# Taking the first adaLN vectors of a two-layer diffusion backbone off GpSimd

## The chip, the cores and the metric

One core of a Trainium2 chip. The metric is the device time of one execution in microseconds (us), the median of several runs. The engines are TensorE (PE in the profile; PEld its weight loads), VectorE (DVE), ScalarE (ACT), GpSimd (POOL) and SyncE (SP), whose queue issues nearly all the loads.

## The reference

Two layers over 512 latent tokens and 256 context tokens of width 1024, in fp32. Each layer is a half-step SwiGLU feed-forward, a token mixer (differential attention in layer 0, windowed grouped-query attention in layer 1) and a second half-step feed-forward. Every one of the six takes its input normalised and modulated:

```
mod_l = (silu(c) @ ada_w[i] + ada_b[i])          # 9 vectors of 1024 for the latent tokens
mod_c = silu(c_ctx) @ ada_w[i] + ada_b[i]        # 9 for the context tokens
h     = rms(t) * (1 + scale) + shift
t     = t + 0.5 * gate * ((silu(h @ wi_gate) * (h @ wi_up)) @ wo)
```

Nine vectors of 1024 for two kinds of token in each layer are a product of a vector with a 1024 x 9216 matrix. The first feed-forward needs the first two, the shift and the scale (columns 0 to 2047), before it can multiply anything; all others are due later. The change concerns those two.

## The kernel before, in words

Activations stand with the 1024 features on the partitions, as 8 chunks of 128, and the 768 tokens along the row. Every large product is taken three times in fp32r, on a rounded part and its remainder of both operands (`split`, L72: ScalarE rounds, VectorE subtracts; the names are `whi`/`wlo` for weights and `h_h`/`h_l` for activations), which gives VectorE much to do everywhere. The program is written through a framework that sets the order of each engine's instructions from its own estimate of times, so a changed part reorders its neighbourhood; `keep` pins an instruction to the written order on its engine.

**The first phase** runs from the start to the first products of the first feed-forward (L1082 to L1141). It does four things:

- `ada_vectors` (L118) spreads `c` and `c_ctx` over all partitions (`crep`, 128 x 2 x 1024) and applies SiLU.
- The norm: ScalarE squares `x` (L1108), VectorE adds the 8 chunks in a tree (L1111), and `rstd_steps` (L277) sums over the partitions on TensorE (`ps_rt`), takes the power -0.5 on GpSimd (L290), makes a diagonal on VectorE (`dg`, L295) and spreads it with a product with ones (`ps_r`, L303). ScalarE copies that to `rall`. Then `xr<-x,rall` (L1122) is the normalised chunk.
- The vectors, `vectors(k)` (L1118) for each chunk k: `ada_job` (L175) loads a 128 x 1024 slab `araw` and takes one row sum for each kind of token. VectorE does the latent one (L187, multiply with an accumulating sum); GpSimd multiplies for the context one (L190) and ScalarE sums that product (L199). All 8 shifts and the scales of chunks 0, 1, 5 and 7 go this way. The scales of chunks 2, 3, 4 and 6 (`ONPE`) go through `scale_job` (L209): 8 products on TensorE in which the 128 x 128 weight block stands still and the two conditions (`cvec`, 2 columns) move past it. The slabs share 6 rooms (`FIRST`).
- `feed(k)` (L1124): ScalarE applies shift and scale (L1134), rounds to `h_h` (L1135), VectorE makes `h_l` (L1136). `ffn` (L500) calls it before the 12 products of chunk k of its first step f = 0 (`products`, L519, matmuls on L522): 6 with 512 columns, 6 with 256. The first four of a chunk need `h_h` only, the other eight need `h_l` or `wlo`.

After f = 0, VectorE multiplies gate and up (`sg`, L555), and the steps f = 1 and f = 2 follow as plain products. From f = 3 on the products are taken in Strassen's form (`Seven`, L397), for which VectorE first adds and subtracts the quarters of the activations (`sums`, L411) and of the weights (`s`, L442 to L445). Beside all this `Halves` (L219) computes the later adaLN vectors on VectorE, six half slabs `wh` per step (L253).

Of the kernel before, what the change touches and what calls it, by code (L numbers as in the profile page):

```python
# [17 lines left out]
P = 128  # L18
D = 1024
# [23 lines left out]
def hybrid_backbone_kernel(ctx: ExitStack, tc: tile.TileContext, I, out):  # L43
# [10 lines left out]
    def one(name, tag="one"):  # L54
        return ps1.tile([P, 512], F32, name=name, tag=tag)
# [62 lines left out]
    def ada_vectors(pool):  # L118

        crep = pool.tile([P, 2, D], F32, name="crep")  # L120
        for ty, nm in enumerate(("c", "c_ctx")):
            nc.sync.dma_start(crep[:, ty], I[nm].partition_broadcast(P))
            nc.scalar.activation(crep[:, ty], crep[:, ty], AF.Silu)
        nc.sync.dma_start(adab, I["ada_b"])
        return crep

    def load_x(half):
        s0, n, _, _ = half
        for d in range(0, KC, 4):
            nc.sync.dma_start(x[:, d:d + 4, s0:s0 + n], I["x"][:, d:d + 4, s0:s0 + n])  # L130

    def load_small():
        nc.scalar.dma_start(ident, I["ident"])
# [36 lines left out]


    mods = [[None] * NMOD for _ in range(2)]
    JUNK, PRODS = 3, 3

    def ada_job(l, j, engines, pool, crep, bufs, pin=False):  # L175
        m, d = divmod(j, KC)
        w = pool.tile([P, D], F32, name="araw", tag="araw", bufs=bufs)
        nc.sync.dma_start(w, I["ada_w"][l, j])
        if mods[l][m] is None:
            md = const.tile([P, 2, KC], F32, name=f"mod{l}_{m}")  # L180
            mods[l][m] = md[:, 0], md[:, 1], md
        prods = []
        for ty in range(2):
            acc = mods[l][m][ty][:, d:d + 1]
            if engines[ty] is nc.vector:
                o = pool.tile([P, D], BF16, name="junk", tag="junk", bufs=JUNK)
                i = nc.vector.scalar_tensor_tensor(o, w, 1.0, crep[:, ty], ALU.mult, ALU.mult, accum_out=acc)  # L187
            else:
                pr = pool.tile([P, D], F32, name="aprod", tag="aprod", bufs=PRODS)
                i = nc.gpsimd.tensor_mul(pr, w, crep[:, ty])  # L190
                prods.append((pr, acc))
            if pin:
                keep(i)
        md = mods[l][m][2][:, :, d]

        def finish():
            for pr, acc in prods:
                o = pool.tile([P, D], BF16, name="junk", tag="junk", bufs=JUNK)
                nc.scalar.activation(o, pr, AF.Identity, accum_out=acc)  # L199
            bias = adab[:, l, j:j + 1].broadcast_to([P, 2])  # L200
            if m in (1, 4, 7):
                nc.vector.scalar_tensor_tensor(md, md, 1.0, bias, ALU.add, ALU.add)
            else:
                nc.vector.tensor_add(md, md, bias)
                if m in (2, 8):
                    nc.vector.tensor_scalar_mul(md, md, 0.5)
        return finish

    def scale_job(k, pool, bufs):  # L209

        w = pool.tile([P, D], F32, name="araw", tag="araw", bufs=bufs)
        nc.sync.dma_start(w, I["ada_s"][k])
        ps = one("ps_a", "acc")[:, :2]
        for i in range(KC):
            nc.tensor.matmul(ps, w[:, i * P:(i + 1) * P], cvec[:, i], start=i == 0, stop=i == KC - 1)
        bias = adab[:, 0, KC + k:KC + k + 1].broadcast_to([P, 2])
        return lambda: nc.vector.scalar_tensor_tensor(mods[0][1][2][:, :, k], ps, 1.0, bias, ALU.add, ALU.add)

    class Halves:  # L219

# [871 lines left out]
    cvec = start.tile([P, KC, 2], F32, name="cvec")  # L1092
    nc.sync.dma_start(cvec, I["cvec"])
    nc.scalar.activation(cvec, cvec, AF.Silu)
    crep = ada_vectors(start)
    md = const.tile([P, 2, KC], F32, name="mod0_1")
    mods[0][1] = md[:, 0], md[:, 1], md
    with tc.tile_pool(name="f0", bufs=1) as pool:
        load_small()
        for hf in range(2):  # L1100
            load_x(all_[hf])
        xr = [pool.tile([P, T], F32, name="xr", tag=("ah", "al")[d % 2], bufs=5) for d in range(KC)]
        rall = pool.tile([P, T], F32, name="rall", tag="ah", bufs=5)
        steps = []
        for s0, n, _, _ in all_:
            tk = slice(s0, s0 + n)
            for d in range(KC):
                nc.scalar.activation(xr[d][:, s0:s0 + n], x[:, d, s0:s0 + n], AF.Square)  # L1108
            for step in (1, 2, 4):
                for d in range(0, KC, 2 * step):  # L1110
                    nc.vector.tensor_add(xr[d][:, s0:s0 + n], xr[d][:, s0:s0 + n], xr[d + step][:, s0:s0 + n])  # L1111
            steps.append(rstd_steps(xr[0][:, tk], n, D, lambda pr, _, tk=tk: nc.scalar.copy(rall[:, tk], pr), pool))
        for z in zip(*steps):
            for step in z:
                step()
        rest = {}

        def vectors(k):  # L1118
            rest[k] = [ada_job(0, k, (V, G), start, crep, FIRST, pin=k == 0),
                       scale_job(k, start, FIRST) if k in ONPE else  # L1120
                       ada_job(0, KC + k, (V, G), start, crep, FIRST, pin=k == 0)]
            keep(nc.vector.tensor_mul(xr[k], x[:, k], rall))  # L1122

        def feed(k):  # L1124

            if k == 0:
                for f in rest.pop(0):
                    f()
            if 0 < k < KC - 1:
                vectors(k + 1)  # L1130
            hi, lo = h0.reg.hi[:, k], h0.reg.lo[:, k]
            for s0, n, ty, _ in all_:
                sh, sc = (mods[0][i][ty][:, k:k + 1] for i in range(2))
                nc.scalar.activation(xr[k][:, s0:s0 + n], xr[k][:, s0:s0 + n], AF.Identity, bias=sh, scale=sc)  # L1134
            nc.scalar.copy(hi, xr[k])  # L1135
            nc.vector.tensor_sub(lo, xr[k], hi.bitcast(F32))  # L1136
            for f in rest.pop(k + 1, ()):
                f()
        vectors(0)
        vectors(1)  # L1140
        h1 = Norm(0, 3, T, "right", "h1_")  # L1141

        def up_done():
            h0.reg.close()
            h1.open()
        halves.add(0, (2,))
# [135 lines left out]
```

## Time and profile before

| | |
|---|---|
| median of 3 runs | 2940.08 us (2938.19 to 2943.32) |
| the profiled execution | 2939.59 us, of which the span from first to last instruction is 2937.8 us |
| TensorE busy | 2733.8 us (93%) |
| VectorE busy | 2229.2 us (76%) |
| ScalarE busy | 1229.8 us (42%) |
| GpSimd busy | 498.3 us (17%) |
| mean granted TensorE clock | 0.979 |

The profile is one execution. "Busy" is the time in which an instruction of the engine is under way. A busy VectorE may still be waiting inside an instruction, and successive instructions overlap by some 0.08 us, so what one costs is read from the distance between two starts. Nothing but the first 5% of the span is touched by the change, and only that stretch is looked at closely. Times in the trace count from the start of the span.

### The profile page before, as it was taken

The numbers are of one execution on the slowest core, as the hardware profiler recorded it, in microseconds if no ns is written. First come the engines' busy times: TensorE is split into PE (matmuls) and PEld (weight loads), VectorE is DVE, ScalarE is ACT, GpSimd is POOL, SyncE is SP. The second block draws the span as 40 slices with busy tenths as digits, with TensorE's granted clock in tenths as the row PEclk, the third lists the DMA queues.
The fourth block names the chain that finished last, engine by engine and source line by source line (L and its number), as shares of the span: only waits on it lengthen the run. The fifth ranks groups of instructions, "written<-read, shape, count | busy, mean of one in ns | idle before, by whom it ended". The sixth has DMA issues, their size and how long they took to land.

```text
span 2937.8 us, 47517 instructions
## 1 busy us (share of the span) xinstructions
PE 2733.8 (93%) x17948; PEld 2589.0 (88%) x17948; DVE 2229.2 (76%) x4613; ACT 1229.8 (42%) x3053; POOL 498.3 (17%) x586
## 2 busy tenths in 40 slices
PE   4799899999999989799999989999999999999999
PEld 3698898889999978789999978999998999999999
DVE  7988987877677756877886598787766766488887
ACT  4423222336556644323333343332334566454443
POOL 5300000025433422200000051000002521220000
PEclk9899999999999999899999999999999999999999
DMA  6333433322011022233332223343322101223333
GB/s 209 114 127 129 133 125 101 119 79 73 30 30 34 26 85 73 86 108 115 109 114 65 72 76 115 126 133 112 100 73 89 45 29 30 73 78 101 98 93 101
DMA packets 98709, 266.49 MB, mean 91 GB/s; under 512 B 12592, under 2 KB 16688, under 8 KB 98352
## 3 DMA queue, kind: packets, MB, share of 16 engines
q1 hardware_dynamic: 91968, 251.78, 26.8%
q10 hardware_dynamic: 6512, 11.68, 1.2%
q8 instruction: 141, 2.31, 0.3%
q14 instruction: 88, 0.72, 0.1%
HBM read 256.07 MB, written 7.34 MB: 90 GB/s over the span
## 4 chain that ended last, share of the span: by engine, by line
PE 66%; DVE 22%; issue 4%; DMA 4%; ACT 2%; POOL 1%; SPq 0%; ACTq 0%; DVEq 0%; POOLq 0%
PE ps_up L456 24%; PE ps_dn L569 22%; PE ps_qkv L651 7%; DVE wlo L74 4%; PE ps_dn L728 4%; DVE wh L253 3%; DVE junkh L253 2%; PE ps_av L989 2%; PE ps_up L522 2%; DMA wh<-in_ada_w 2%; DVE xs L369 1%; DMA raw<-in_pre_wi 1%; PE ps_av L825 1%; PE ps_s L781 1%; PE ps_pt L978 1%
## 5 line engine op out<-in xcount | busy, mean ns | idle before, releaser
L73 ACT CAST whi<-raw 128x512 fp32r<-128x512 f32 x556 | 341.4, 620 | 765.5 <-PE ps_dn L569 318.0
L569 PE MATMUL ps_dn<-ah,whi 128*128 128x256 f32 (+1 forms) x1456 | 463.3, 321 | 2.6 <-DVE x L390 1.8
L74 DVE TENSOR_TENSOR wlo<-raw,whi 128x512 fp32r<-128x512 f32 x556 | 402.9, 729 | 79.9 <-ACT whi L73 68.4
L569 PE MATMUL ps_dn<-al,whi 128*128 128x256 f32 (+1 forms) x1456 | 462.0, 319 | 0.1
L569 PE MATMUL ps_dn<-ah,wlo 128*128 128x256 f32 (+1 forms) x1456 | 454.1, 319 | 0.2 <-DVE wlo L74 0.2
L456 PE MATMUL ps_up<-h_h,whi 128*128 128x384 f32 (+1 forms) x1216 | 400.9, 330 | 38.7 <-ACT whi L73 25.9
L456 PE MATMUL ps_up<-h_h,wlo 128*128 128x384 f32 (+1 forms) x1216 | 394.3, 328 | 12.9 <-DVE wlo L74 12.8
L456 PE MATMUL ps_up<-h_l,whi 128*128 128x384 f32 (+1 forms) x1216 | 397.8, 327 | 0.0
L390 DVE SCALAR_TENSOR_TENSOR x<-ps_dn,mod,x 128x256 f32<-128x256 f32 (+1 forms) x442 | 241.9, 556 | 142.5 <-PE ps_dn L569 101.9
L73 ACT CAST whi<-s 128x512 fp32r<-128x512 f32 x304 | 188.1, 620 | 266.9 <-PE ps_up L456 221.9
L569 PEld LDWEIGHTS ps_dn<-ah,whi 128*128 128x128 f32 x1456 | 276.1, 191 | 25.3 <-ACT whi L73 2.5
L569 PEld LDWEIGHTS ps_dn<-al,whi 128*128 128x128 f32 x1456 | 277.5, 191 | 19.6 <-DVE al L74 0.3
L569 PEld LDWEIGHTS ps_dn<-ah,wlo 128*128 128x128 f32 x1456 | 275.9, 191 | 19.4 <-DVE wlo L74 0.4
L456 PEld LDWEIGHTS ps_up<-h_h,whi 128*128 128x128 f32 x1216 | 233.1, 192 | 47.1 <-ACT whi L73 27.2
L456 PEld LDWEIGHTS ps_up<-h_h,wlo 128*128 128x128 f32 x1216 | 232.2, 192 | 15.1 <-DVE wlo L74 15.0
L74 DVE TENSOR_TENSOR wlo<-s,whi 128x512 fp32r<-128x512 f32 x304 | 208.2, 687 | 41.7 <-ACT whi L73 38.0
L456 PEld LDWEIGHTS ps_up<-h_l,whi 128*128 128x128 f32 x1216 | 233.0, 192 | 0.5
L651 PE MATMUL ps_qkv<-whi,h_h 128*128 128x256 f32 x704 | 205.4, 292 | 4.3 <-DVE a L607 3.6
L651 PE MATMUL ps_qkv<-wlo,h_h 128*128 128x256 f32 x704 | 199.7, 286 | 1.9 <-DVE wlo L74 1.9
L651 PE MATMUL ps_qkv<-whi,h_l 128*128 128x256 f32 x704 | 200.3, 285 | 0.0
L257 POOL TENSOR_TENSOR mod<-mod,part 128x16 f32<-128x16 f32 (+1 forms) x32 | 14.7, 460 | 1065.4 <-DVE wh L253 1031.5
L253 DVE SCALAR_TENSOR_TENSOR wh<-wh,ch 128x512 f32<-128x512 f32 x256 | 185.5, 733 | 1.7 <-DMA wh<-in_ada_w 1.5
(226 smaller groups left out, 6684.9 us busy)
## 6 DMA issues: line engine op xcount, KB each, us to landing
wh<-in_ada_w SPq DMA_DIRECT2D x256, 256.0 KB, 3.7
raw<-in_pre_wi SPq DMA_DIRECT2D x88, 512.0 KB, 3.5
raw<-in_post_wi SPq DMA_DIRECT2D x88, 512.0 KB, 3.5
raw<-in_pre_wo SPq DMA_DIRECT2D x44, 512.0 KB, 3.5
raw<-in_post_wo SPq DMA_DIRECT2D x44, 512.0 KB, 3.5
raw<-in_a_w_qk SPq DMA_DIRECT2D x16, 512.0 KB, 3.5
araw<-in_ada_w SPq DMA_DIRECT2D x12, 512.0 KB, 4.5
raw<-in_a_w_v SPq DMA_DIRECT2D x8, 512.0 KB, 3.5
```

The costliest lines, as they stand in the source:

```text
L73: nc.scalar.copy(hi, src)
L74: nc.vector.tensor_sub(lo, src, hi.bitcast(F32))
L253: nc.vector.scalar_tensor_tensor(o, w, 1.0, self.c[ty], ALU.mult, ALU.mult, accum_out=self.part[:, ty, d:d + 1])
L369: nc.vector.scalar_tensor_tensor(xs, x[:, d, tk], sc, self.r[p], ALU.mult, ALU.mult)
L390: nc.vector.scalar_tensor_tensor(x[:, d, s0:s0 + n], ps, gate[ty][:, d:d + 1], x[:, d, s0:s0 + n], ALU.mult, ALU.add)
L456: nc.tensor.matmul(ps, ww, z[:, k, :n], start=first and k == 0 and i == 0, stop=k == 3 and i == 2, skip_group_check=True)
L522: nc.tensor.matmul(ps, w, h[:, k, s0:s0 + n], start=k == 0 and i == 0, stop=k == KC - 1 and i == 2)
L569: nc.tensor.matmul(ps, wv, a[:, s0:s0 + n], start=fi == 0 and k == 0, stop=fi == nf - 1 and k == 2)
L651: nc.tensor.matmul(ps, h[:, k, bt], w, start=n == 0, stop=n == 23)
L728: nc.tensor.matmul(ps, wv, o[:, k, s0:s0 + n], start=k == 0 and j == 0, stop=k == KC - 1 and j == 2)
L781: nc.tensor.matmul(sv[:, u], Q[:, c, qt], K[:, c, kb0 * P + u * half:kb0 * P + (u + 1) * half], start=i == 0, stop=i == 1)
L989: nc.tensor.matmul(po[:, j], a[:, k, j], V[:, kb, g], start=k == 0, stop=k == len(kbs) - 1)
```

## The change

All 16 shift sums go to VectorE, two accumulating multiplies a chunk, each chunk's load followed by its sums at once. All 8 scales go to TensorE, and there the operands change places: the two conditions stand still (2 columns of weights) and the 128 columns of the weight block move. The result is a 2 x 128 row, which ScalarE copies out of the accumulator (`row`) and a small product with a 2 x 2 identity turns back into two columns (`ps_b`). GpSimd keeps only the power of the norm. The first two shift slabs are loaded ahead of `x`, the first two scale slabs behind it, all pinned to that order; the slabs have 9 rooms.

```diff
     def load_x(half):
         s0, n, _, _ = half
         for d in range(0, KC, 4):
-            nc.sync.dma_start(x[:, d:d + 4, s0:s0 + n], I["x"][:, d:d + 4, s0:s0 + n])
+            keep(nc.sync.dma_start(x[:, d:d + 4, s0:s0 + n], I["x"][:, d:d + 4, s0:s0 + n]))
...
-    def ada_job(l, j, engines, pool, crep, bufs, pin=False):
-        m, d = divmod(j, KC)
+    def shift_job(k, pool, crep, bufs):
         w = pool.tile([P, D], F32, name="araw", tag="araw", bufs=bufs)
-        nc.sync.dma_start(w, I["ada_w"][l, j])
...
-            if engines[ty] is nc.vector:
-                o = pool.tile([P, D], BF16, name="junk", tag="junk", bufs=JUNK)
-                i = nc.vector.scalar_tensor_tensor(o, w, 1.0, crep[:, ty], ALU.mult, ALU.mult, accum_out=acc)
-            else:
-                pr = pool.tile([P, D], F32, name="aprod", tag="aprod", bufs=PRODS)
-                i = nc.gpsimd.tensor_mul(pr, w, crep[:, ty])
-                prods.append((pr, acc))
...
-                nc.scalar.activation(o, pr, AF.Identity, accum_out=acc)
...
+        keep(nc.sync.dma_start(w, I["ada_w"][0, k]))
+        md = mods[0][0][2][:, :, k]
+
+        def sums():
+            for ty in range(2):
+                o = w if ty else pool.tile([P, D], BF16, name="junk", tag="junk", bufs=2)
+                nc.vector.scalar_tensor_tensor(o, w, 1.0, crep[:, ty], ALU.mult, ALU.mult, accum_out=md[:, ty:ty + 1])
+            nc.vector.tensor_add(md, md, adab[:, 0, k:k + 1].broadcast_to([P, 2]))
+        return sums
 
     def scale_job(k, pool, bufs):
         w = pool.tile([P, D], F32, name="araw", tag="araw", bufs=bufs)
-        nc.sync.dma_start(w, I["ada_s"][k])
-        ps = one("ps_a", "acc")[:, :2]
-        for i in range(KC):
-            nc.tensor.matmul(ps, w[:, i * P:(i + 1) * P], cvec[:, i], start=i == 0, stop=i == KC - 1)
-        bias = adab[:, 0, KC + k:KC + k + 1].broadcast_to([P, 2])
-        return lambda: nc.vector.scalar_tensor_tensor(mods[0][1][2][:, :, k], ps, 1.0, bias, ALU.add, ALU.add)
+        keep(nc.sync.dma_start(w, I["ada_s"][k]))
+
+        def sums():
+            ps = one("ps_a", "acc")
+            for i in range(KC):
+                nc.tensor.matmul(ps[:2, :P], cvec[:, i], w[:, i * P:(i + 1) * P], start=i == 0, stop=i == KC - 1)
+            row = pool.tile([2, P], F32, name="row", tag="row", bufs=2)
+            nc.scalar.copy(row, ps[:2, :P])
+            pt = one("ps_b", "acc")[:, :2]
+            nc.tensor.matmul(pt, row, ident[:2, :2], start=True, stop=True)
+            bias = adab[:, 0, KC + k:KC + k + 1].broadcast_to([P, 2])
+            nc.vector.scalar_tensor_tensor(mods[0][1][2][:, :, k], pt, 1.0, bias, ALU.add, ALU.add)
+        return sums
...
-    FIRST = 6
-    ONPE = (2, 3, 4, 6)
-    V, G = nc.vector, nc.gpsimd
+    FIRST = 9
...
+        crep = ada_vectors(start)
+        shifts = [shift_job(k, start, crep, FIRST) for k in range(2)]
+        keep(nc.sync.dma_start(adab, I["ada_b"]))
         for hf in range(2):
             load_x(all_[hf])
+        scales = [scale_job(k, start, FIRST) for k in range(2)]
+        for f in shifts:
+            f()
...
+        for f in scales:
+            f()
+        later = {}
 
         def feed(k):
 
-            if k == 0:
-                for f in rest.pop(0):
-                    f()
-            if 0 < k < KC - 1:
-                vectors(k + 1)
+            if k + 2 < KC:
+                later[k + 2] = [shift_job(k + 2, start, crep, FIRST), scale_job(k + 2, start, FIRST)]
             hi, lo = h0.reg.hi[:, k], h0.reg.lo[:, k]
+            nc.vector.tensor_mul(xr[k], x[:, k], rall)
             for s0, n, ty, _ in all_:
...
-            for f in rest.pop(k + 1, ()):
+            for f in later.get(k + 2, ()):
                 f()
```

**Where the instructions stand.** VectorE from the last tree addition to the first normalised chunk, before (`junk` is a latent sum of a shift, `mod_0`, or a scale, `mod_1`):

```order
L295 TENSOR_TENSOR dg<-ident,r 128x512
L74 TENSOR_TENSOR wlo<-raw,whi 128x512
L295 TENSOR_TENSOR dg<-ident,r 128x256
L187 SCALAR_TENSOR_TENSOR junk,mod_0_176<-araw,crep 128x1024
L187 SCALAR_TENSOR_TENSOR junk,mod_1_100<-araw,crep 128x1024
L187 SCALAR_TENSOR_TENSOR junk,mod_0_176<-araw,crep 128x1024
L74 TENSOR_TENSOR wlo<-raw,whi 128x512 x3
L187 SCALAR_TENSOR_TENSOR junk,mod_1_100<-araw,crep 128x1024
L1122 TENSOR_TENSOR xr<-x,rall 128x768 x2
```

The same place of the change (line numbers are those of the changed kernel; the sums that write `araw` are those of the context tokens):

```order
L74 TENSOR_TENSOR wlo<-raw,whi 128x512 x3
L273 TENSOR_SCALAR v<-ps_rt 128x4
L74 TENSOR_TENSOR wlo<-raw,whi 128x512
L182 SCALAR_TENSOR_TENSOR junk,mod_0_94<-araw,crep 128x1024
L273 TENSOR_SCALAR v<-ps_rt 128x2
L201 SCALAR_TENSOR_TENSOR mod_1_95<-ps_b,adab 128x2
L280 TENSOR_TENSOR dg<-ident,r 128x512
L182 SCALAR_TENSOR_TENSOR araw,mod_0_94<-araw,crep 128x1024
L182 SCALAR_TENSOR_TENSOR junk,mod_0_94<-araw,crep 128x1024
L183 TENSOR_TENSOR mod_0_94<-mod_0_94,adab 128x2
L280 TENSOR_TENSOR dg<-ident,r 128x256
L201 SCALAR_TENSOR_TENSOR mod_1_95<-ps_b,adab 128x2
```

The weights' remainders now stand ahead of the norm's `v` and `dg`, and the scales' results (`mod_1` from `ps_b`) stand between them. A little further on in the change, up to the first `h_l`:

```order
L201 SCALAR_TENSOR_TENSOR mod_1_95<-ps_b,adab 128x2
L1114 TENSOR_TENSOR xr<-x,rall 128x768 x4
L182 SCALAR_TENSOR_TENSOR araw,mod_0_94<-araw,crep 128x1024
L1114 TENSOR_TENSOR xr<-x,rall 128x768 x4
L182 SCALAR_TENSOR_TENSOR junk,mod_0_94<-araw,crep 128x1024
L201 SCALAR_TENSOR_TENSOR mod_1_95<-ps_b,adab 128x2
L182 SCALAR_TENSOR_TENSOR junk,mod_0_94<-araw,crep 128x1024
L1119 TENSOR_TENSOR h_l<-xr,h_h 128x768
```

All eight chunks are normalised ahead of the first `h_l`, where before chunks and sums took turns. TensorE from its first matmul to the first products, before:

```order
L286 MATMUL ps_rt<-ones,xr 128x1 x6
L303 MATMUL ps_r<-dg,ones 128x512
L303 MATMUL ps_r<-dg,ones 128x256
L215 MATMUL ps_a<-cvec,araw 128x2 x24
L522 MATMUL ps_up<-h_h,whi 128x512 x2
L522 MATMUL ps_up<-h_h,whi 128x256 x2
L215 MATMUL ps_a<-cvec,araw 128x2 x8
```

and in the change:

```order
L195 MATMUL ps_a<-araw,cvec 2x128 x8
L271 MATMUL ps_rt<-ones,xr 128x1 x6
L199 MATMUL ps_b<-ident,row 128x2
L195 MATMUL ps_a<-araw,cvec 2x128 x8
L288 MATMUL ps_r<-dg,ones 128x512
L199 MATMUL ps_b<-ident,row 128x2
L195 MATMUL ps_a<-araw,cvec 2x128 x8
L288 MATMUL ps_r<-dg,ones 128x256
L199 MATMUL ps_b<-ident,row 128x2
L195 MATMUL ps_a<-araw,cvec 2x128 x8
L199 MATMUL ps_b<-ident,row 128x2
L195 MATMUL ps_a<-araw,cvec 2x128 x8
```

Scale products now stand ahead of both of the norm's steps, and five of the eight scales stand ahead of the first products of f = 0; the sixth stands behind the first four products of chunk 0, the last two inside chunks 3 and 5.

## Rows read from the trace of the kernel before

**Rows 1.** The page: the span, and its chain by engine.

```profile
span 2937.8 us, 47517 instructions
...
PE 66%; DVE 22%; issue 4%; DMA 4%; ACT 2%; POOL 1%; SPq 0%; ACTq 0%; DVEq 0%; POOLq 0%
```

**Rows 2.** Stretches, all engines (10 to 20 us) and VectorE alone: length, busy, clock, DMA share, GB/s.

```profile
10.00:20.00 10.00, 1.22 (x6) 1.22 (x6) 6.58 (x13) 6.83 (x16) 1.29 (x8) 1.00 1.06 388
...
89.40:145.10 55.70, 54.88 (x100) 0.86 0.33 102
```

**Rows 3.** Chain of waits, 0 to 140 us: start us, us, what.

```profile
78.11 17.97 PE ps_up L522 x87
96.08 0.61 DVE junkh L253 x2
```

**Rows 4.** Groups by shape, 0 to 90 us: count | busy, mean ns | idle before.

```profile
L190 POOL TENSOR_TENSOR aprod<-araw,crep 128x1024 f32<-128x1024 f32 x12 | 34.3, 2881 | 13.5 <-ACT junk L199 13.5
L187 DVE SCALAR_TENSOR_TENSOR junk<-araw,crep 128x1024 bf16<-128x1024 f32 x12 | 20.2, 1708 | 0.0
...
L1122 DVE TENSOR_TENSOR xr<-x,rall 128x768 f32<-128x768 f32 x8 | 13.9, 1753 | 0.0
...
L74 DVE TENSOR_TENSOR wlo<-raw,whi 128x512 fp32r<-128x512 f32 x6 | 9.1, 1551 | 1.2 <-ACT whi L73 1.2
...
L204 DVE TENSOR_TENSOR mod<-mod,adab 128x2 f32<-128x2 f32 x8 | 7.6, 953 | 0.0
```

**Rows 5.** Timeline of VectorE, 0 to 110 us: start us, us, line, operation [idle before].

```profile
31.27 1.21 DVE L187 SCALAR_TENSOR_TENSOR junk<-araw,crep 128x1024 bf16<-128x1024 f32 x1
...
46.83 0.15 DVE L204 TENSOR_TENSOR mod<-mod,adab 128x2 f32<-128x2 f32 x1
...
48.19 0.95 DVE L1122 TENSOR_TENSOR xr<-x,rall 128x768 f32<-128x768 f32 x1
...
83.50 0.95 DVE L1136 TENSOR_TENSOR h_l<-xr,h_h 128x768 fp32r<-128x768 f32 x1
...
89.41 0.69 DVE L555 TENSOR_TENSOR sg<-sg,ps_up 128x512 f32<-128x512 f32 x1 [1.90 <-ACT sg L554]
90.02 0.69 DVE L74 TENSOR_TENSOR wlo<-raw,whi 128x512 fp32r<-128x512 f32 x1
```

**Rows 6.** Timeline of TensorE, 0 to 110 us and near 800 us.

```profile
18.78 2.94 PE L286 MATMUL ps_rt<-ones,xr 128*128 128x1 f32 x12 [18.78 <-DVE xr L1111]
22.88 2.05 PE L303 MATMUL ps_r<-dg,ones 128*128 128x512 f32 x2 [1.16 <-DVE dg L295]
...
55.13 3.55 PE L215 MATMUL ps_a<-cvec,araw 128*128 128x2 f32 x16 [0.80 <-DMA araw<-in_ada_s]
58.61 0.79 PE L522 MATMUL ps_up<-h_l,whi 128*128 128x512 f32 x1
...
61.33 1.48 PE L522 MATMUL ps_up<-h_h,whi 128*128 128x512 f32 x4
...
80.84 1.09 PE L522 MATMUL ps_up<-h_h,whi 128*128 128x512 f32 x4
...
83.18 0.86 PE L522 MATMUL ps_up<-h_h,whi 128*128 128x512 f32 x4
...
85.30 0.86 PE L522 MATMUL ps_up<-h_h,whi 128*128 128x512 f32 x4
...
89.52 0.40 PE L522 MATMUL ps_up<-h_h,whi 128*128 128x512 f32 x1
...
800.00 1.60 PE L825 MATMUL ps_av<-V,aT 128*128 128x128 f32 x12
```

**Rows 7.** Timeline of ScalarE, 0 to 110 us.

```profile
11.21 2.19 ACT L1108 ACTIVATE xr<-x 128x512 f32<-128x512 f32 x4 [2.00 <-DMA x<-in_x]
13.93 4.64 ACT L1108 ACTIVATE xr<-x 128x512 f32<-128x512 f32 x12 [0.53 <-DMA x<-in_x]
23.32 1.14 ACT L73 CAST whi<-raw 128x512 fp32r<-128x512 f32 x2 [4.75 <-DMA raw<-in_pre_wi]
```

More of the change, by code (lines that the diff above doesn't have):

```diff
@@ L123, in ada_vectors @@
             nc.scalar.activation(crep[:, ty], crep[:, ty], AF.Silu)
-        nc.sync.dma_start(adab, I["ada_b"])
         return crep
@@ L172, in hybrid_backbone_kernel @@
     mods = [[None] * NMOD for _ in range(2)]
-    JUNK, PRODS = 3, 3
-    def ada_job(l, j, engines, pool, crep, bufs, pin=False):
-        m, d = divmod(j, KC)
+    def shift_job(k, pool, crep, bufs):
         w = pool.tile([P, D], F32, name="araw", tag="araw", bufs=bufs)
-        nc.sync.dma_start(w, I["ada_w"][l, j])
[L179 to L184, printed above, removed]
-            if engines[ty] is nc.vector:
-                o = pool.tile([P, D], BF16, name="junk", tag="junk", bufs=JUNK)
-                i = nc.vector.scalar_tensor_tensor(o, w, 1.0, crep[:, ty], ALU.mult, ALU.mult, accum_out=acc)
-            else:
-                pr = pool.tile([P, D], F32, name="aprod", tag="aprod", bufs=PRODS)
-                i = nc.gpsimd.tensor_mul(pr, w, crep[:, ty])
-                prods.append((pr, acc))
[L192 to L198, printed above, removed]
-                nc.scalar.activation(o, pr, AF.Identity, accum_out=acc)
[L200 to L207, printed above, removed]
@@ L1094, in hybrid_backbone_kernel @@
     nc.scalar.activation(cvec, cvec, AF.Silu)
-    crep = ada_vectors(start)
-    md = const.tile([P, 2, KC], F32, name="mod0_1")
-    mods[0][1] = md[:, 0], md[:, 1], md
+    for m in range(2):
+        md = const.tile([P, 2, KC], F32, name=f"mod0_{m}")
+        mods[0][m] = md[:, 0], md[:, 1], md
     with tc.tile_pool(name="f0", bufs=1) as pool:
         load_small()
+        crep = ada_vectors(start)
+        shifts = [shift_job(k, start, crep, FIRST) for k in range(2)]
+        keep(nc.sync.dma_start(adab, I["ada_b"]))
         for hf in range(2):
             load_x(all_[hf])
+        scales = [scale_job(k, start, FIRST) for k in range(2)]
+        for f in shifts:
+            f()
         xr = [pool.tile([P, T], F32, name="xr", tag=("ah", "al")[d % 2], bufs=5) for d in range(KC)]
@@ L1115, in hybrid_backbone_kernel @@
                 step()
[L1116 to L1122, printed above, removed]
-        def feed(k):
-            if k == 0:
-                for f in rest.pop(0):
-                    f()
-            if 0 < k < KC - 1:
-                vectors(k + 1)
+        for f in scales:
+            f()
+        later = {}
+        def feed(k):
+            if k + 2 < KC:
+                later[k + 2] = [shift_job(k + 2, start, crep, FIRST), scale_job(k + 2, start, FIRST)]
             hi, lo = h0.reg.hi[:, k], h0.reg.lo[:, k]
+            nc.vector.tensor_mul(xr[k], x[:, k], rall)
             for s0, n, ty, _ in all_:
@@ L1136, in feed @@
             nc.vector.tensor_sub(lo, xr[k], hi.bitcast(F32))
-            for f in rest.pop(k + 1, ()):
+            for f in later.get(k + 2, ()):
                 f()
-        vectors(0)
-        vectors(1)
         h1 = Norm(0, 3, T, "right", "h1_")
```

## The prediction

> **What bounds the kernel now.** I read the page first, then the chain of waits of the first 140 us, then the groups and timelines of that stretch. The page says that TensorE ends 66% of the chain and VectorE 22% [rows 1]; the change touches only the first feed-forward's start, so what matters is who ends the waits there. Up to 78 us it is nearly always VectorE. Then TensorE takes the chain without a wait for 18 us, and at 96.08 it goes back to VectorE [rows 3], which works almost without a pause until it has the quarters for step f = 3: from 89.4 to 145.1 us it is busy 54.88 of 55.70 us [rows 2]. That stretch opens with the first `sg`, at 89.41 [rows 5], and it starts there because f = 0 then ends on TensorE (f = 1 follows at 89.52 [rows 6]). So the end of f = 0 is the number to move. What it moves by, everything behind moves by: VectorE's list from `sg` to the first weights of f = 3 is the same before and after but for one sum more (28 half-slab sums instead of 27), and from there the engines' orders nearly coincide.
>
> **What VectorE gets back.** Before 90 us its instructions come in two lengths. A sum takes 1.21 us when alone, a normalised chunk 0.95, a weights' remainder 0.69, the addition of a bias 0.15 [rows 5]. The means are 1708, 1753, 1551 and 953 ns [rows 4]. The excess is 12 x 0.50 + 8 x 0.80 + 6 x 0.86 + 8 x 0.80 = 24 us, and next to it stand 12 GpSimd multiplications of 2881 ns mean [rows 4]. I read the excess as VectorE waiting inside its instructions for GpSimd's operands. The change takes those multiplications away, so the 24 us go. It adds four sums of VectorE (16 for 12, 1.14 us from start to start), 4.6 us, and takes away little else. VectorE's own list in this phase gets some 19 to 20 us shorter.
>
> ScalarE loses 12 sums and gets 8 short copies; it had idle time and I cost it at nothing, except where TensorE waits for a copy (below).
>
> **What the loads do.** The order puts two shift slabs (0.524 MB each) ahead of `x`. At the 388 GB/s of the stretch from 10 to 20 us [rows 2] that is 1.35 us a slab, so the two parts of `x` that started ScalarE at 11.21 and 13.93 come 2.7 us later, at 13.9 and 16.6. The first weights came at 23.32 behind four slabs [rows 7] and still have four ahead of them: 23.3. The two scale slabs right before them land at 20.6 and 22.0, and each slab behind is 1.35 us on; the last lands near 41 us. By the list of uses below a room is always free in time, so 9 rooms hold nothing up.
>
> **What TensorE gets.** This is the other side. It took four scales of 3.55 us [rows 6]; now it takes eight, and in its queue they stand ahead of the norm's steps and of the first products. What one costs in the new form no row shows. It is still 16 passes. From below, 12 fp32 passes with 128 columns took 1.60 us near 800 us, where TensorE runs at 2.4 GHz [rows 6]: 2.1 us at most for 16. From above, two passes of 512 columns took 2.05 us early on [rows 6], a quarter of it for 128 columns is 0.26 a pass and 4.1 us for 16. At the lower clock I take 3.55, the old form's price, which lies between, and half of it, 1.8, at the higher. The small product behind each I put at 0.4 us.
>
> Which clock? The spacing of the products shows the two levels. Four products of chunk 1 took 1.48 us at 61.33, and 0.86 at 83.18 [rows 6]: 1.2 and 2.4 GHz. A chunk of 12 costs 2.12 us at the higher level (83.18 to 85.30) and about 4.0 at the lower (2.72 for eight, 58.61 to 61.33, and 1.3 for four) [rows 6]. The granted clock of 1.00 in the early stretch [rows 2] does not show this; I go by the spacing. TensorE rose at 80.84, where four products take 1.09 [rows 6], after working without a wait from 78.11 [rows 3]. From 55.13 to 62.8 it had also worked without a wait, first 3.55 us on a scale, then on products, and stayed at the lower level [rows 6].
>
> **The sum.** At the lower level, in the order of TensorE's queue: scale 0 from 20.6 to 24.2; the norm's sums 2.94 us [rows 6], 27.1; small product 27.5; scale 1, 31.0; spread of 512 columns 2.05, 33.1; small product and scale 2, 37.0; spread of 256, about 1.1, 38.1; small product and scale 3, 42.1; again with scale 4, 46.0; the first four products 47.3; again with scale 5, 51.3; the other eight products of chunk 0, 54.0.
>
> VectorE is not late in this list. Its first normalised chunk waits for scale 2 and stands at 38.6; eight chunks at 0.87 and three sums at 1.14 bring the first `h_l` to 49.9, ahead of 51.3. Behind it eight `h_l` and four sums are 11.5 us. So TensorE sets the end, and once products stand behind each other with no wait, as from 78.11 before, I let it rise: at 54. Then chunks 1 to 7 take 14.8 us, two scales 3.6, three small products 1.2, and the last chunk's wait for its scale, through VectorE and ScalarE, about 1: f = 0 ends at 74.6 instead of 89.5. That is 14.9 us, less 0.6 for the one sum more: 14.3. From the profiled 2939.6 us that gives **2925.3**; the median of the runs stands 0.5 above the profiled one, so I keep 2925.
>
> **Rivals.** *The clock rises early.* TensorE works from 20.6 us on nearly without a pause. If the scale passes bring it to 2.4 GHz by about 33 us, scales 2 to 5 cost 1.8 each and VectorE is the bound: with the norm spread at 36 its first `h_l` comes at 47.7, and from there 1.4 + 14.8 + 3.6 + 1.2 + 1 us of TensorE end f = 0 at 69.7. The gain is 19.8 less 0.6, the time 2920.4. For it: an almost unbroken queue. Against it: the 7.7 us from 55.13, half of them scale passes, at the lower level. The Trainium skill ("TensorE: Matmul & The Clock Gate", Part 1) says that the lower clock is the resting state and that sustained matmul activity releases it. By that rule this case is the one to expect; the trace agrees from 78.11 on and not from 55.13 on. Chance 0.32.
>
> *The clock never rises, or the gain is given back behind.* With no rise, 54.0 + 28 + 7.1 + 1.2 ends f = 0 at 90.3, against 89.5 before: 2941, no change. Against it: products without a wait did raise the clock at 80.84. A wait for loads behind `sg` would come to the same, but there VectorE idled only 0.8 of 55.7 us [rows 2]. Chance 0.12.
>
> *ScalarE's copies hold TensorE.* This one ends on the slow side. Every small product waits for ScalarE to copy the row, and in ScalarE's queue the copies of scales 3 to 7 stand behind the activations and the cast of a chunk. At 0.55 us for 512 columns [rows 7] three passes over 768 columns are some 2 us. If TensorE stands still that long for six scales, and therefore stays at 1.2 GHz, f = 0 ends at 90.3 + 12 = 102, the time is 2952. It decides as soon as the clock stays low, because the sum without any rise has no room left. For it: the in-order queues, and in the early case I already find 2.5 us of such waits. Against it: in the list above the copies are ready in time except one or two. Chance 0.06.
>
> **How the numbers follow.** My own case has 0.50: with the scale's price between its two ends (2.1 to 4.1 us) and the rise some us sooner or later it spans 2920 to 2931. The early case spans 2913 to 2921. Together they reach down to 2911, if VectorE gets all its 24 us back and TensorE follows at once, and the range goes up to 2940, into the case of no change. What a measurement can tell from no change here is about 0.2%, 5.9 us. Faster by more than that: both rising cases, 0.82. Within it: 0.12. Slower: 0.06.
>
> **What would show it.** In the changed profile: sums of 1.21 us, normalised chunks of 0.95 and bias additions of 0.15 throughout, with no long ones; 16 sums on VectorE; GpSimd with nothing but the norm's power before 70 us; the first `h_l` near 50; products spaced for 2.4 GHz soon after 54; the first `sg` near 75; and the list from `sg` to the first weights of f = 3 still some 56 us long. I am wrong if long VectorE instructions remain, if products stay at the lower spacing to the end of f = 0, if TensorE waits for copies between scales for more than some 3 us in all, or if `sg` comes early and f = 3 does not.

## The result, and the profile after the change

| | median | runs | ratio to before, 95% interval |
|---|---|---|---|
| before, beside it | 2941.70 us | 2938.19 to 2944.16 (4) | |
| after | 2924.37 us | 2923.03 to 2926.32 (4) | 0.9942 [0.9925, 0.996] |

The kernel is faster by some 17 us, 0.6%, well beyond the 0.2% that a measurement tells from no change. The profiled execution took 2926.32 us, with a span of 2924.5 us, 13.3 us less than the one before [rows 1].

The page of the changed kernel, its span and its chain by engine:

```profile
span 2924.5 us, 47636 instructions
...
PE 67%; DVE 20%; DMA 4%; issue 4%; ACT 3%; POOL 1%; SPq 0%; DVEq 0%; ACTq 0%; POOLq 0%
```

VectorE gave two points of the chain back. Its groups of the first 90 us, in the columns of [rows 4], and after them its timeline, in those of [rows 5]:

```profile
L182 DVE SCALAR_TENSOR_TENSOR araw<-araw,crep 128x1024 f32<-128x1024 f32 x8 | 9.7, 1217 | 0.1
L182 DVE SCALAR_TENSOR_TENSOR junk<-araw,crep 128x1024 bf16<-128x1024 f32 x8 | 9.7, 1217 | 9.3 <-DMA araw<-in_ada_w 9.3
...
L1114 DVE TENSOR_TENSOR xr<-x,rall 128x768 f32<-128x768 f32 x8 | 7.1, 950 | 0.0
...
L74 DVE TENSOR_TENSOR wlo<-raw,whi 128x512 fp32r<-128x512 f32 x9 | 6.0, 686 | 0.8 <-ACT whi L73 0.8
...
L183 DVE TENSOR_TENSOR mod<-mod,adab 128x2 f32<-128x2 f32 x8 | 1.2, 154 | 0.0
```

```profile
36.73 3.56 DVE L1114 TENSOR_TENSOR xr<-x,rall 128x768 f32<-128x768 f32 x4
...
41.35 3.56 DVE L1114 TENSOR_TENSOR xr<-x,rall 128x768 f32<-128x768 f32 x4
...
45.98 0.15 DVE L201 SCALAR_TENSOR_TENSOR mod<-ps_b,adab 128x2 f32<-128x2 f32 x1
...
47.19 0.95 DVE L1119 TENSOR_TENSOR h_l<-xr,h_h 128x768 fp32r<-128x768 f32 x1
...
49.07 2.52 DVE L1119 TENSOR_TENSOR h_l<-xr,h_h 128x768 fp32r<-128x768 f32 x1
...
72.89 0.69 DVE L540 TENSOR_TENSOR sg<-sg,ps_up 128x512 f32<-128x512 f32 x1 [0.26 <-ACT sg L539]
...
78.55 6.81 DVE L405 TENSOR_TENSOR both<-h_h,h_l 128x768 f32<-128x768 f32 x3
...
129.84 0.68 DVE L74 TENSOR_TENSOR wlo<-s,whi 128x512 fp32r<-128x512 f32 x1
```

The means of [rows 4] (1708, 1753, 1551 and 953 ns) have become 1217, 950, 686 and 154: every one is now the length that the instruction has alone. The first `sg` starts at 72.89 instead of 89.41 [rows 5], 16.5 us sooner. The list behind it, up to the first weights of f = 3, takes 56.95 us (before 55.72), so that point comes 15.3 us sooner, and 13.3 of it reach the end.

TensorE's timeline, in the columns of [rows 6]:

```profile
21.62 3.57 PE L195 MATMUL ps_a<-araw,cvec 128*2 128x128 f32 x16 [21.62 <-DMA araw<-in_ada_s]
25.12 2.72 PE L271 MATMUL ps_rt<-ones,xr 128*128 128x1 f32 x12
...
28.28 3.58 PE L195 MATMUL ps_a<-araw,cvec 128*2 128x128 f32 x16
...
33.75 1.91 PE L195 MATMUL ps_a<-araw,cvec 128*2 128x128 f32 x16
...
39.23 0.38 PE L199 MATMUL ps_b<-ident,row 2*128 2x2 f32 x2 [0.79 <-ACT row L197]
...
41.38 0.97 PE L507 MATMUL ps_up<-h_h,whi 128*128 128x512 f32 x4
43.25 0.38 PE L199 MATMUL ps_b<-ident,row 2*128 2x2 f32 x2 [0.91 <-ACT row L197]
46.18 3.13 PE L195 MATMUL ps_a<-araw,cvec 128*2 128x128 f32 x16 [2.55 <-DVE mod L201]
...
51.14 0.86 PE L507 MATMUL ps_up<-h_h,whi 128*128 128x512 f32 x4
```

Two scales of 3.57 us are at 1.2 GHz; from 33.75 on a scale takes 1.91, the pace of 2.4 GHz. Then, at 46.18, one scale takes 3.13 again, behind a wait of 2.55 us for the bias addition at 45.98. Stretches of TensorE (length, busy, granted clock, DMA share, GB/s) bear that fall out, but not the slow start:

```profile
20.00:34.00 14.00, 12.38 (x53) 1.00 1.02 408
34.00:46.00 12.00, 7.93 (x60) 1.00 0.87 295
46.00:51.00 5.00, 4.82 (x23) 0.66 0.01 2
```

The granted clock reads 1.00 from 20 to 34 us, where two scales ran at about half their later pace. Here too the length of the passes is the better witness.

### The profile page after: what moved, and what is told of

Read it like the earlier page. It is cut to its first block, busy times and chain, and to the rows that moved or that the text cites. A ratio compares the mean times of both kernels' runs of the same rounds, so it can differ in the third digit from the quotient of the medians.

```text
span 2924.5 us, 47636 instructions
## 1 busy us (share of the span) xinstructions
PE 2731.0 (93%) x18028; PEld 2577.5 (88%) x18028; DVE 2215.3 (76%) x4621; ACT 1218.6 (42%) x3037; POOL 466.0 (16%) x574
## 4 chain that ended last, share of the span: by engine, by line
PE 67%; DVE 20%; DMA 4%; issue 4%; ACT 3%; POOL 1%; SPq 0%; DVEq 0%; ACTq 0%; POOLq 0%
PE ps_up L441 24%; PE ps_dn L554 22%; PE ps_qkv L636 7%; DVE wlo L74 4%; PE ps_dn L713 4%; DVE wh L238 2%; DVE junkh L238 2%; PE ps_av L974 2%; DMA raw<-in_post_wi 1%; DVE xs L354 1%; DMA wh<-in_ada_w 1%; PE ps_up L507 1%; PE ps_av L810 1%; PE ps_s L766 1%; PE ps_pt L963 1%
```

## The experiments

Two theories went in. **Waits inside VectorE:** the gain is GpSimd's multiplications gone; scales and rooms only follow. Its rival, **TensorE:** the gain is the clock that rises early because the new scales keep TensorE at work. And a third question, what the wait at 46 us and the late rise still cost. All runs in a table; the ratio is to the kernel before, timed beside it; `sg` and f = 3 are the starts of the first `sg` and of the first `wlo<-s` (before: 89.41 and 145.13). The medians come from all runs of a kernel, `sg` and f = 3 from its one profiled execution. Behind f = 3 two profiled executions of the same kernel, the change and e5, alike there to 0.1 us, end 4.0 us apart (spans 2924.5 and 2920.5 us); what a shift of some us at f = 3 makes of the end can't be read from one execution.

| kernel | median, us (runs) | ratio, 95% interval | `sg` | f = 3 |
|---|---|---|---|---|
| weights stand still (e1) | 2929.25 (7) | 0.9954 [0.9939, 0.9969] | 72.76 | 129.07 |
| six rooms (e2) | 2920.44 (4) | 0.9928 [0.9909, 0.9947] | 71.21 | 128.16 |
| before, sums on VectorE (e3) | 2928.09 (5) | 0.9959 [0.9942, 0.9976] | 76.69 | 132.16 |
| GpSimd beside (e4) | 2941.68 (10) | 1.0002 [0.999, 1.0014] | 96.35 | 153.31 |
| the change again (e5) | 2920.93 (6) | 0.9931 [0.9916, 0.9945] | 72.93 | 129.91 |
| small products in other banks (e6) | 2914.10 (4) | 0.9911 [0.9893, 0.993] | 66.19 | 120.55 |
| warmed (e7) | 2921.25 (4) | 0.9932 [0.9913, 0.995] | 74.16 | 131.13 |
| warmed, other banks, six rooms (e8) | 2915.91 (5) | 0.9916 [0.99, 0.9931] | 65.08 | 120.68 |
| six rooms again (e9) | 2921.53 (4) | 0.9936 [0.9916, 0.9957] | 70.38 | 127.35 |
| other banks, six rooms (e10) | 2918.49 (6) | 0.9924 [0.9909, 0.9938] | 69.33 | 123.69 |
| before, all scales on TensorE (e11) | 2939.95 (10) | 0.9999 [0.9987, 1.0011] | 81.06 | 138.00 |

### GpSimd's share: e3, e4 and e11

e3 is the kernel before with one thing changed: VectorE takes GpSimd's and ScalarE's 12 sums too.

```diff
-            rest[k] = [ada_job(0, k, (V, G), start, crep, FIRST, pin=k == 0),
+            rest[k] = [ada_job(0, k, (V, V), start, crep, FIRST, pin=k == 0),
...
-                       ada_job(0, KC + k, (V, G), start, crep, FIRST, pin=k == 0)]
+                       ada_job(0, KC + k, (V, V), start, crep, FIRST, pin=k == 0)]
```

> The kernel before with one edit: the 12 sums that GpSimd multiplied and ScalarE summed go to VectorE, which now does 24 sums; scales on TensorE, rooms and loads as before. My theory: VectorE loses 24 us of waits inside its instructions and gains 12 x 1.14 = 13.7 us of work; the first sg comes about 10 us ahead of 89.4, at 78 to 82, time 2930 to 2934. Rival (the gain came from the loads and their order, or from the scales on TensorE): sg stays at 87 or later, or with 13.7 us of work more on a full VectorE goes to 95 to 103, time 2940 to 2955.

VectorE's groups of the first 90 us in e3:

```profile
L187 DVE SCALAR_TENSOR_TENSOR junk<-araw,crep 128x1024 bf16<-128x1024 f32 x24 | 30.3, 1282 | 0.0
L1122 DVE TENSOR_TENSOR xr<-x,rall 128x768 f32<-128x768 f32 x8 | 7.6, 950 | 0.0
...
L204 DVE TENSOR_TENSOR mod<-mod,adab 128x2 f32<-128x2 f32 x8 | 1.2, 152 | 0.0
```

VectorE got 12 sums more, 12 x 1.14 = 13.7 us of work, and its first `sg` came 12.7 us *sooner*, earlier still than I had expected. Chunks and bias additions fell to the lengths they have alone, as in the changed kernel, a sum to 1282 ns in the mean. By the medians it is worth 13.6 us to take GpSimd's products away, and ScalarE's sums with them; e4 separates the two.

e4 puts the multiplications back into the changed kernel: 12 of the same size, on the same slabs, whose results nothing reads. Nothing is left out of the computation. Both sums write to `junk`, since GpSimd still reads the slab; there are 8 rooms.

```diff
 def shift_job(k, pool, crep, bufs):
+            pr = pool.tile([P, D], F32, name="aprod", tag="aprod", bufs=1)
+            nc.gpsimd.tensor_mul(pr, w, crep[:, 1])
...
-                o = w if ty else pool.tile([P, D], BF16, name="junk", tag="junk", bufs=2)
+                o = pool.tile([P, D], BF16, name="junk", tag="junk", bufs=2)
...
 def scale_job(k, pool, bufs):
+            if k in (0, 1, 5, 7):
+                pr = pool.tile([P, D], F32, name="aprod", tag="aprod", bufs=1)
+                nc.gpsimd.tensor_mul(pr, w, crep[:, 1])
```

> The changed kernel with 12 GpSimd multiplications of a slab put back beside it, at the 8 shift slabs and 4 of the scale slabs; nobody reads their results (8 rooms, for space). My theory: each holds VectorE inside an instruction for up to 2.2 us; VectorE's instructions of 3.1 to 3.4 us come back, some 15 to 25 us in all, of which its slack behind 46 us (about 10 us of waits for TensorE and ScalarE) hides a part: first sg at 80 to 90, time 2932 to 2941. Rival (VectorE's waits were not due to GpSimd): sg within 2 us of 72.9, time within 3 us of the changed kernel's.

The groups of e4 from 18 to 72 us, two bias additions of its timeline and GpSimd's multiplications beside them, and TensorE's waits from 18 to 96 us:

```profile
L181 POOL TENSOR_TENSOR aprod<-araw,crep 128x1024 f32<-128x1024 f32 x7 | 18.8, 2687 | 0.3
L184 DVE SCALAR_TENSOR_TENSOR junk<-araw,crep 128x1024 bf16<-128x1024 f32 x10 | 18.2, 1852 | 0.0
...
L185 DVE TENSOR_TENSOR mod<-mod,adab 128x2 f32<-128x2 f32 x4 | 4.8, 1189 | 0.0
```

```profile
45.19 0.15 DVE L206 SCALAR_TENSOR_TENSOR mod<-ps_b,adab 128x2 f32<-128x2 f32 x1
45.26 2.23 DVE L185 TENSOR_TENSOR mod<-mod,adab 128x2 f32<-128x2 f32 x1
41.84 5.64 POOL L181 TENSOR_TENSOR aprod<-araw,crep 128x1024 f32<-128x1024 f32 x2
```

```profile
PE ps_b L204 <- DVE mod L206: 8.5, 2, 6.4
PE ps_r L293 <- DVE dg L285: 5.8, 1, 5.8
PE ps_a L200 <- DVE mod L206: 3.5, 1, 3.5
```

No instruction of VectorE waits for these multiplications by a semaphore, yet sums and bias additions are back at the lengths of [rows 4]; one addition to 2 columns takes 2.23 us, alone 0.15. It ends at 47.49, and GpSimd's multiplications beside it end at 47.48. The addition right ahead of it, at 45.19, takes 0.15 us in the midst of the same multiplications; one of its two inputs, `ps_b`, lies in the accumulator. All 8 of that kind take 0.15 to 0.16 us in e4. The first `sg` is 23.5 us later, past the 80 to 90 I had expected, because TensorE now waits 17.8 us for VectorE as well. It waits for no slab behind the first (at 21.8 us, in the change at 21.6), so late loads are not the cause, and ScalarE did not get its sums back, so they were not the gain. The whole gain is gone: 1.0002 [0.999, 1.0014].

e11 is the counterpart: the kernel before with all eight scales on TensorE in their old form, and GpSimd kept for the 8 shifts.

```diff
-    ONPE = (2, 3, 4, 6)
+    ONPE = tuple(range(KC))
```

> The kernel before with one edit: all 8 scales on TensorE in the old form; the 8 shifts stay as they were, the latent sums on VectorE and the context ones on GpSimd and ScalarE. VectorE loses 4 sums (4.6 us) and 4 of 12 waits for GpSimd (about 8 us). My theory: the end of f = 0 goes with VectorE's list, the first sg comes 8 to 13 us ahead of 89.4, at 76.5 to 81.5, with 8 long VectorE instructions left; time 2928 to 2934. Rival: TensorE's four more scales of 3.5 us are on the path as long as it stays at 1.2 GHz; sg at 84 or later, time 2936 or more.

Groups of e11 to 90 us, and TensorE's wait for the bias additions from 10 to 84 us:

```profile
L190 POOL TENSOR_TENSOR aprod<-araw,crep 128x1024 f32<-128x1024 f32 x8 | 23.5, 2956 | 9.4 <-DMA araw<-in_ada_w 9.4
L187 DVE SCALAR_TENSOR_TENSOR junk<-araw,crep 128x1024 bf16<-128x1024 f32 x8 | 13.9, 1748 | 0.0
...
L204 DVE TENSOR_TENSOR mod<-mod,adab 128x2 f32<-128x2 f32 x8 | 7.0, 882 | 0.0
```

```profile
PE ps_a L215 <- DVE mod L217: 11.4, 3, 6.4
```

Four GpSimd multiplications fewer leave VectorE's sums and bias additions about as long as before (1748 and 882 ns for 1708 and 953; the chunks fall to 1484, the weights' remainders to 686), and TensorE waits 11.4 us for VectorE. In the profiled execution `sg` comes at 81.06, 8.3 us sooner and as expected, but that was the fastest of ten (2932.45); the median gives nothing, 0.9999 [0.9987, 1.0011]. Why the others do not show those 8 us is open. e3 and e4 show that GpSimd's absence is the gain. Without it the scales on TensorE bring nothing by the median; what they add beside it lies within the 4 to 7 us between e3 and the change, from which no run separates the order of the loads.

### The form of the scales, and the rooms: e1, e2 and e9

e1 keeps the changed kernel but turns the operands back: the weight block stands still, two columns move, no row, no small product.

```diff
-                nc.tensor.matmul(ps[:2, :P], cvec[:, i], w[:, i * P:(i + 1) * P], start=i == 0, stop=i == KC - 1)
-            row = pool.tile([2, P], F32, name="row", tag="row", bufs=2)
-            nc.scalar.copy(row, ps[:2, :P])
-            pt = one("ps_b", "acc")[:, :2]
-            nc.tensor.matmul(pt, row, ident[:2, :2], start=True, stop=True)
+                nc.tensor.matmul(ps, w[:, i * P:(i + 1) * P], cvec[:, i], start=i == 0, stop=i == KC - 1)
```

> The changed kernel, but all 8 scales in the old form: the weight blocks stand still, the 2 columns of the conditions move; no row copy, no small product. My theory: the new form (128 moving columns) is what took TensorE to 2.4 GHz by 33 us in the changed kernel; in the old form it stays at 1.2 GHz through the scales, each costs 3.5 us to the last one ahead of the products, the rise comes only among the products, and the first sg comes 2 to 4 us later than 72.9, near 75 to 77; time 2926 to 2929. Rival: the form does not matter for the clock, or the saved copies and small products pay for it: scales of 1.8 us from about 33 us on, first sg at 70 to 73, time 2921 to 2925.

TensorE in e1, timeline and stretches:

```profile
40.16 6.83 PE L195 MATMUL ps_a<-cvec,araw 128*128 128x2 f32 x32
...
49.20 3.57 PE L195 MATMUL ps_a<-cvec,araw 128*128 128x2 f32 x16 [0.72 <-DVE mod L197]
...
64.75 1.84 PE L195 MATMUL ps_a<-cvec,araw 128*128 128x2 f32 x16
```

```profile
20.00:34.00 14.00, 12.74 (x57) 1.00 1.03 410
34.00:52.00 18.00, 17.28 (x74) 1.00 0.52 193
```

Half of each side was right. The passes stay at 0.21 us, 1.2 GHz, through seven of the eight scales, although TensorE is busy for 17.28 of 18 us; the products behind them come to the pace of 2.4 GHz only at 57.7, and the last scale, at 64.75, takes 1.84 us. In the new form the rise came at 33, among the scales. The form also changed the order of TensorE's list, so e1 doesn't show that it was the form alone. But `sg` is no later, 72.76: without the copies TensorE waits only once, for 0.72 us, and it earns in waits what it loses in pace. By the medians the new form is worth 5 to 8 us, but the intervals meet, and what e1 loses in its profile (a span of 2928.3 us for 2924.5) it loses behind f = 3, where the change and e5 differ by nearly as much. What the form is worth stays open.

e2, and e9 again, take the rooms away (`FIRST = 6` for 9).

> The changed kernel with 6 rooms for the slabs instead of 9; the orders of the engines are otherwise the same. My theory: a room is nearly always free in time, because a slab is used within some 10 us of its landing; the first sg stays within 1.5 us of 72.9 and the time within 2 us of the changed kernel's 2924. Rival: the rooms carry a part of the gain: the loads of scales 4 to 7 come too late for TensorE's queue, TensorE waits for loads by 3 us or more, sg comes at 76 or later, time 2928 or more.

> The changed kernel with 6 rooms, once more. In the two executions with 9 rooms TensorE rose near 33 us and the first sg stood at 72.9; in the one with 6 rooms it rose near 25 us, sg at 71.2. If the moment of the rise hangs on the rooms: rise near 25 again, sg at 71.2 within 0.3. If it is a matter of the execution: rise and sg elsewhere, 71 to 73.5. The time in both cases 2918 to 2924, within the spread of the changed kernel's two medians (2920.9 and 2924.4).

Both are level with the change or a little ahead (2920.44 and 2921.53 against 2924.37 and 2920.93). Rooms carry nothing, as the prediction had it.

### What was left on the table: e5, e6, e10, e7 and e8

e5 is the change once more beside these kernels.

> The changed kernel itself once more, on the same chip and beside the next three. In its first execution TensorE rose to 2.4 GHz near 33 us, while with 6 rooms, the orders being the same, it rose near 25 us and sg came 1.7 us sooner. My theory: the moment of the rise differs from execution to execution, not from room count to room count; so the first sg lies anywhere between 71 and 75 us and the median between 2920 and 2926. Rival: the rooms (and where the slabs lie) make the difference; sg again at 72.9 within 0.3, the median again 4 us above that of 6 rooms, 2924 or more.

It repeats: `sg` at 72.93, the rise of the clock at about 33 us again, as the rival had it; the median, 2920.93, is that of my theory.

e6 gives the small product a bank of the norm's kind. In the change it shares two banks (`acc`) with the scales.

```diff
-            pt = one("ps_b", "acc")[:, :2]
+            pt = one("ps_b")[:, :2]
```

> The changed kernel, with the small product's result in the other pair of accumulator banks (those of the norm). My theory: in the changed kernel scale 5 waited 2.55 us for a bank, since both banks of its pair held results that VectorE read only behind the eight normalised chunks; that wait let TensorE fall to 1.2 GHz and cost some 1.3 us more. With banks of its own the wait of 2.55 us and the fall at 46 us go, the first sg comes at 68 to 70.5, time 2920 to 2922. Rival: TensorE only waits at another place (for the first h_l, near 47), sg stays within 1 us of the changed kernel's of the same call.

TensorE in e6: its timeline, one stretch, and its longest wait between 24 and 72 us:

```profile
24.32 1.05 PE L271 MATMUL ps_rt<-ones,xr 128*128 128x1 f32 x8
...
26.58 3.00 PE L195 MATMUL ps_a<-araw,cvec 128*2 128x128 f32 x26
...
42.30 1.91 PE L195 MATMUL ps_a<-araw,cvec 128*2 128x128 f32 x16
...
51.63 1.48 PE L507 MATMUL ps_up<-h_h,whi 128*128 128x512 f32 x4
```

```profile
52.00:54.00 2.00, 2.00 (x7) 0.50 0.00 0
```

```profile
PE ps_b L199 <- DVE mod L201: 1.6, 1, 1.6
```

The scale no longer waits for a bank, `sg` comes 6.7 us sooner than in e5, and the median is 2914.10 against e5's 2920.93 beside it. The fall of the clock is not gone, though, it comes later: behind a wait of 1.6 us that ends at 49.16, the granted clock is 0.50 from 52 to 54, and four products take 1.48 us at 51.63. This is the lowest median of the study: some 28 us under the kernel before, 0.9911 [0.9893, 0.993]. It gained more than I had expected, for two reasons. The scales now run ahead of the small products, an order that the one line brought with it; and the clock had risen by 24 us, which it also did in e2 and e9 without that line.

e10 is e6 with six rooms, to see whether the rooms set that moment.

> The changed kernel with the small product's result in the norm's banks and 6 rooms, without the products of ones. By the theory that the wait for a bank was the costly one: first sg at 65.5 to 68, time 2912 to 2917, as with 9 rooms (2914.1). Rival (the 2914 was a lucky build): 2919 or more.

TensorE in e10, at the places of the first two lines of e6:

```profile
24.54 1.87 PE L271 MATMUL ps_rt<-ones,xr 128*128 128x1 f32 x8
...
28.65 5.24 PE L195 MATMUL ps_a<-araw,cvec 128*2 128x128 f32 x26
```

TensorE does the same work in the same order as in e6, and here the rise comes at 33 instead of 24: the 8 norm sums take 1.87 for 1.05, the 26 passes 5.24 for 3.00. `sg` is 3.1 us later for it. Nine rooms rose at 33 in two profiles and at 24 in e6; six at 24 to 25 in e2 and e9 and at 33 in e10. So it is not the rooms; and the two kernels that were profiled twice (the change and e5, e2 and e9) each rose at the same place both times. What decides the moment is open. So the line is priced between kernels with the same rise, across the room counts: with the rise at 33, `sg` moves from 72.9 to 69.33 (e10), 3.6 us; with the rise at 24, from 71.21 and 70.38 (e2, e9) to 66.19 (e6), 4.2 to 5.0. In the medians it is 6.8 us (e5 to e6) and 3.0 us (e9 to e10), each time with ranges that overlap a little.

e7 tries to be early by force: 80 products of ones with ones, read by nothing, before the first slab (an addition, nothing is left out). e8 adds the same to e10.

```diff
+    wm = one("ps_w")
+    for _ in range(80):
+        nc.tensor.matmul(wm[:, :P], ones, ones, start=True, stop=True)
```

> The changed kernel with 80 products of ones with ones on TensorE ahead of the first scale, from about 1 to 20 us, results unread. My theory: TensorE reaches the first scale at 2.4 GHz, so scales 0 and 1, the norm's sums and its spread cost 1.9, 1.9, 1.5 and 1.1 instead of 3.5, 3.5, 2.7 and 1.7: up to 5 us sooner, of which the loads of scale 2 and VectorE's sums leave 2 to 4; first sg at 68.5 to 71, time 2920 to 2922. Rival: the loads or VectorE set the start of the normalised chunks anyway, sg within 1 us of the changed kernel's of the same call.

> The changed kernel with both: the small products in the norm's banks and the 80 products of ones ahead; 6 rooms. If both theories hold: first sg at 65 to 68.5, and all behind comes as much sooner: 2916 to 2919. If TensorE then waits for VectorE's first h_l and the loads instead: sg at 69 to 71, 2920 to 2922.

TensorE from its first scale, in e7 and then in e8:

```profile
23.43 2.09 PE L195 MATMUL ps_a<-araw,cvec 128*2 128x128 f32 x14 [2.82 <-DMA araw<-in_ada_s]
25.45 1.87 PE L271 MATMUL ps_rt<-ones,xr 128*128 128x1 f32 x8
...
29.22 3.57 PE L195 MATMUL ps_a<-araw,cvec 128*2 128x128 f32 x16
```

```profile
21.87 1.69 PE L195 MATMUL ps_a<-araw,cvec 128*2 128x128 f32 x14 [0.47 <-DMA araw<-in_ada_s]
```

In e7 the clock falls within the first scale, behind 2.82 us of waiting for its slab: 14 passes take 2.09 us, where e8 has 1.69, the norm's sums behind them run at the lower pace (1.87 us for 8), and the next scale takes 3.57 again. The slab also landed 2 us later than in e5 (23.43 for 21.25), and `sg` came at 74.16, not at the 68.5 to 71 I had expected. Warming gains nothing by itself (2921.25, beside 2920.93). In e8 the wait for that slab is 0.47 us, the clock holds, and `sg` is the soonest of all, 65.08; its median is within 2 us of e6, so nothing is added to it that can be told apart.

## Why the prediction held

Forecast 2925 (2911 to 2940), measured 2924.37 and, timed again in e5, 2920.93. The direction and the cause were right. That the number came out to a microsecond is luck. In TensorE's list two errors nearly cancelled: the early rise of the clock, worth 4.9 us by the rival's sum, and 3.3 us more behind it, in part a wait that I did not have; so f = 0 ended at 73.0 for my 74.6. And the gain itself is known less well than that: 13.3 us between the two profiled executions, where I had 14.3, but 17.3 and 21.1 us between the medians.

- **VectorE's waits inside its instructions: right.** All four groups fell to the lengths they have alone. e3 shows the cause by taking GpSimd out of the old kernel and e4 by putting it back into the new one. Up to `sg` one long instruction was left, the `h_l` of 2.52 us at 49.07: the scheduler gave GpSimd one of Strassen's additions at 48.29. "GpSimd only the power before 70" was wrong by that one, and by its copies of biases. Behind `sg` such waits go on: three `both` take 6.81 us at 78.55, while GpSimd does two of its own from 79.46; in the kernel before, with GpSimd at rest there, three took 2.69.
- **Loads: right to about a microsecond.** The first scale slab started TensorE at 21.62 (forecast 20.6), `x` started ScalarE at 14.48 and 17.22 (13.9, 16.6), the weights at 24.05 (23.3). Rooms carry nothing (e2, e9).
- **VectorE's list: 1.8 us early.** The first normalised chunk starts at 36.73 for 38.6. From there my own terms (8 x 0.87 + 3 x 1.14) start the first `h_l` at 49.0; the 49.9 that I wrote, like the rival's 47.7, is where it is done. It started at 47.19 and was done at 48.14.
- **What a scale costs: right.** 3.57 and 1.91 us for my 3.55 and 1.8; the small product 0.3 to 0.5 for 0.4.
- **The clock in TensorE's list: this step failed.** I let it rise at 54, among the products; it rose at 33, among the scales, as the first rival had it. The Trainium skill ("TensorE: Matmul & The Clock Gate", Part 1) says that sustained matmul activity releases the lower resting clock; here the trace agrees. In e1, busy for 17.28 of 18 us at 1.2 GHz, it does not, as it did not from 55.13 on in the kernel before [rows 6].
- **The waits: missed, and they paid part of the error back.** By the rival's own sum f = 0 would have ended at 69.7; it ended at 73.0. Of the 3.3 us between, 1.5 stand ahead of the first product that reads `h_l`. The rival has it at 47.7; `h_l` was done at 48.14, but TensorE came to the product only at 49.24, because the scale ahead of it had waited 2.55 us for a bank and then run slow for 1.2. The eight products from there took 1.90 us for 1.4, still part of that fall. The 1.3 left lie among the chunks behind and are not traced. Two banks serve scales and small products. The small results of scales 3 and 4 stood ready from 39.6 and 43.6; VectorE, in its order, read them only at 45.98 and 49.00, behind eight normalised chunks, and the first of these reads let scale 5 start. I had counted waits for ScalarE's copies (1.7 us, within my bound of 3) but not this one. With other banks, and the order that came with them, `sg` is 3.6 to 5.0 us sooner where the clock rises at the same moment (e6, e10).
- **Behind `sg`: nearly right.** The list is 56.95 us, 1.2 longer where I had 0.6. Of the 16.5 us at `sg`, 15.3 are left at f = 3 and 13.3 at the end; the last difference is smaller than the 4.0 us by which two executions of the change itself differ behind f = 3.
- **The rival on the slow side** needed a clock that stays low and 12 us of waits for copies; there were 1.7. (By its own row three passes over 768 columns are 2.5 us, not "some 2", which makes six of them 15.)

## What to carry to other kernels

Compare the length of one kind of VectorE instruction alone and beside GpSimd before counting either engine as full: here VectorE took 13.7 us of GpSimd's work and was done 12.7 us sooner. When a small result is added to a pool of banks, ask not when it is ready but when the engine that reads it gets to it; another bank cost one line and brought 3.6 to 5 us at the first `sg`, 3 to 7 in the medians. And put a list at either clock beside the other: where the end differs little, as here (74.6 or 69.7), the direction doesn't hang on knowing when the clock rises, only on its rising at all (90.3 without).

## What the runs showed of the hardware

- A VectorE instruction can take 2.23 us for 2 columns instead of 0.15, with no semaphore between it and GpSimd's multiplication, and ends as that one ends (47.49 and 47.48, e4). The Trainium skill ("SBUF — State Buffer", Who interferes with whom) says that an instruction of VectorE with two inputs in SBUF and one of GpSimd that reads SBUF exclude each other; e3 and e4 agree. So do e4's additions with one input in the accumulator, which take 0.15 us beside the same multiplications.
- TensorE stayed at 1.2 GHz through seven scales of e1, nearly without a pause, and rose at 57.7 among the products; in the changed kernel, which differs in the form of the scales and in the order that follows from it, it rose at 33, among them. The rise came at 24 us or at 33 in two kernels whose TensorE does the same work in the same order (e6 and e10), and that makes 3 us of `sg`.
- After the wait of 2.55 us at 43.6, in a stretch of short work and waits, the clock fell: granted 0.66 from 46 to 51, a scale 3.13 us for 1.91. That and the slower products behind it cost over half as much again as the wait itself. In e6, which has no such wait, the clock fell later, behind one of 1.6 us (granted 0.50 from 52 to 54); in e8, which never shows a lower pace from its first scale to `sg`, `sg` came soonest.
